# A gated delta-rule mixer: projections cut into halves and emitted between the stages of the inverse and the steps of the scan, decays four heads at a time, squares 512 wide, two output tiles opened in the last scan

## The chip, the cores and the metric

The kernel runs on one core of a Trainium2 chip. A core has a matrix engine (TensorE, "PE" in the profile; "PEld" is its weight load), VectorE ("DVE"), ScalarE ("ACT"), GpSimd ("POOL") and SyncE ("SP"), which run their own streams of instructions and wait for each other by semaphores; transfers between HBM and the on-chip memory SBUF go through queues that SP and POOL fill. The metric is the device time of one launch in microseconds (us). Lower is better. Matrix results land in PSUM, a small memory of eight banks.

## The reference

A trunk of two layers on 512 tokens of width 1024. Each layer is a half-step feed-forward block, a mixer, another half-step feed-forward block, each behind an RMS norm. The first layer's mixer is an attention and convolution hybrid; the second layer's is a gated DeltaNet of eight heads of 128, which alone is touched here. Cut to that:

```python
proj = h @ w_in                                    # q, k, v, z: 8 heads x 128 each; b, a: 8 each
qkv  = silu(causal_depthwise_conv(proj[q, k, v], conv_w))     # 4 taps
beta = sigmoid(b);  g = -exp(a_log) * softplus(a + dt_bias)   # log decay per token and head
# gated_delta_rule(l2_normalize(q), l2_normalize(k), v, g, beta), in chunks:
g     = cumsum(g within a chunk)
decay = exp(where(causal, g[i] - g[j], -inf))
l_mat = where(strict, (k*beta) @ k.T * decay, 0)
t_inv = inverse(l_mat + eye)                       # a triangular inverse per head and chunk
u, w  = t_inv @ (v*beta),  t_inv @ (k*beta*exp(g))
attn  = where(causal, q @ k.T * decay, 0)
for each chunk:                                    # the scan: a state S per head
    v_new = u - w @ S
    o     = (q*exp(g)) @ S + attn @ v_new
    S     = S * exp(g_last) + (k*exp(g_last - g)).T @ v_new
return (rms_norm(o, norm_g) * silu(z)) @ w_out
```

## The kernel before

Everything is float32 to the reader. A product of full accuracy (`mm3`) is made of three matmuls on split operands, high by high, low by high and high by low, at the lines 140, 141 and 142 of the profile. Activations lie transposed: features on the 128 partitions, the 512 tokens along the free axis (`T` = 512, four chunks `c` of 128). A **projection** (`proj`, one head of q, k, v or z) is 8 blocks `k` times 3 matmuls of 128x512, and there are 32 of them. Its weights come by `load_split`: SP loads `raw` from HBM, ACT makes `whi` and `wlo` = -whi (lines 126, 127), and a DMA of POOL's queue adds the weights into `wlo` (line 128, "wlo<-in_wgdn"). `whi` and `wlo` have three buffers each.

Work per pair of heads, in `gdn_heads`:

- `key_pair(pair)`: projections of k, the convolution and SiLU (`conv_silu`; VectorE lines 1034 and 1039, ACT lines 1037 and 1043), transposes on PE (line 1051), sums of squares (`sumsq`, ACT line 1057: for each of four chunks a Square with an accumulator), and after the first pair `decay(hd)` for all eight heads. A `decay` broadcasts a row on PE (line 156), makes `exp` on ACT (1117), a subtraction on VectorE (1120) and four more `exp` on ACT (1122), and stores two tiles to HBM, `Ed` and `Dd`, through POOL's queue (1118, 1123). These tiles are taken from a set of five buffers with the tag `s`, as nearly all passing tiles of the mixer are. Then the pair's `Dd` comes back, k times k is formed (1155), scaled into the strict lower matrix (VectorE, 1158) and stored as `Ld` (1160).
- `substitute(half)`: for four heads at once, 31 rows of forward substitution on VectorE, each a multiply (1178) and a reduction (1179), which invert the 32x32 diagonal blocks. It reads `Ld` and writes `Vd` in HBM (1182).
- `value_query(hd)`: projections of v and q, `vb`, the product q by k (1203), the masked attention `at`.
- `gate(hd)`: the projection of z and its SiLU (1212, 1213).
- `inverse(pair)`: loads `Ld` and `Vd` (1221) and puts the blocks together in four small stages on PE (lines 1229, 1235, 1241/1242, 1249), with VectorE or ACT between.
- `scan(pair)`: four chunks by two heads, each a chain of small matmuls on PE (1263, 1267, 1268, 1273, 1282) with VectorE and ACT between; then sums of squares of the output `po`, a factor `f`, and scaled copies (1298).
- `finish(hd)`: transposes, gate and norm gain (1306), and a split into `o_x[hd]`, an operand of the output projection.
- `out_proj`: eight output tiles `d`, each 8 blocks `k` by 3 matmuls over `o_x[0]` to `o_x[7]`.

The order of instructions within each engine in this part is set by a scheduler at build time: it goes by data and buffers, by its own costs, and by the order in which the code emits the work (earlier is more urgent). It may pull later-emitted work ahead of work that it thinks must wait. Emitted in a row are: keys of pairs 0 and 1, `substitute(0)`, keys of pairs 2 and 3, values and queries of heads 0 and 1, `inverse` of pair 0; then for each pair its `scan`, the next pair's `inverse`, after the first scan `substitute(1)`, the gates of this pair, values and queries of the next, and `finish`. PSUM has two banks for each of the tags `mm`, `po`, `tr` and `sc`.

## Time and profile before

| what | value |
|---|---|
| median of 3 runs | 2097.8 us (2097.16 to 2097.91) |
| the profiled execution, its own time | 2098.93 us |
| its span, first to last instruction | 2097.2 us |
| mean granted TensorE clock | 0.974 of full speed |
| PE busy | 2020.4 us, 96% of the span |
| VectorE busy | 1609.0 us, 77% |
| ScalarE busy | 1113.9 us, 53% |
| the DeltaNet mixer | about 1341 to 1720 us of the span |
| in it, 1341 to 1498 (up to the first inverse) | PE busy 142.24 of 157.00 us, clock 0.97 |
| in it, 1498 to 1585.5 (first inverse to third) | PE busy 80.21 of 87.50 us, clock 0.80 |
| in it, 1585.5 to 1720 | PE busy 134.05 of 134.50 us, clock 0.97 |

A line of a table by windows gives, for a stretch of the span, the busy time of each engine with its count of instructions, then the granted TensorE clock (1.00 is full speed), the busy share of the DMA engines, and what they moved. PE counts as busy too while its matmuls run at a lower clock, so what PE lost is read from both numbers: its idle time, and the clock below 1. A line of a table of waits names the engine and the line that waited, what ended the wait, the sum, the number of times and the longest.

### The profile page before, as it was taken

What the parts mean: (1) busy time and instruction counts of PE and PEld (TensorE: products, weight loads), DVE (VectorE), ACT (ScalarE), POOL (GpSimd) and SP (SyncE); (2) the same over time, 40 slices, a digit from 0 to 9 for tenths busy, and PEclk for the clock granted to TensorE, in tenths of its full rate; (3) what the DMA queues carried; (4) which work ended last, traced back from release to release, by engine and by line L of the source; (5) the groups of instructions that cost most, each with busy time, mean ns of one, the idle gap of its engine ahead of it and who ended that gap; (6) DMA issues with size and microseconds to landing.
All of it is one profiled execution on the core that took longest, in us unless ns stands there. A gap on an engine that the chain in (4) does not pass through costs nothing.

```text
span 2097.2 us, 32970 instructions
## 1 busy us (share of the span) xinstructions
PE 2020.4 (96%) x12694; PEld 1785.7 (85%) x12694; DVE 1609.0 (77%) x2758; ACT 1113.9 (53%) x1981; POOL 134.0 (6%) x190
## 2 busy tenths in 40 slices
PE   7999999999999999998999999979989999999997
PEld 6999998786579999987999998767778878999986
DVE  5888879798567888889888788657585578888876
ACT  5444447547654444465444446676445654444455
POOL 0000000110000000000000000233302210000000
PEclk9999999999899999999999999999889999999998
DMA  3333332784143333322333332679635563333321
GB/s 125 101 103 109 101 100 83 183 194 97 29 101 116 101 104 108 96 86 84 107 104 105 101 101 82 183 215 231 137 106 131 121 132 107 109 101 102 104 87 46
DMA packets 108845, 237.70 MB, mean 113 GB/s; under 512 B 22160, under 2 KB 24976, under 8 KB 108688
## 3 DMA queue, kind: packets, MB, share of 16 engines
q1 hardware_dynamic: 90544, 193.06, 29.7%
q0 software_dynamic: 17616, 42.02, 10.8%
q8 instruction: 99, 1.62, 0.3%
q14 instruction: 58, 0.48, 0.1%
q10 hardware_dynamic: 528, 0.52, 0.1%
HBM read 224.55 MB, written 11.01 MB: 112 GB/s over the span
## 4 chain that ended last, share of the span: by engine, by line
PE 80%; DVE 8%; issue 5%; ACT 3%; DMA 3%; SPq 0%; POOL 0%; DVEq 0%; ACTq 0%; POOLq 0%
PE mm L141 13%; PE mm L140 13%; PE mm L142 13%; PE sc L141 7%; PE sc L140 7%; PE sc L142 7%; PE po L142 3%; PE po L141 2%; PE po L140 2%; PE tr L140 2%; PE tr L142 2%; PE tr L141 2%; DVE wlo L117 1%; DVE gl L386 1%; PE tr L1051 1%
## 5 line engine op out<-in xcount | busy, mean ns | idle before, releaser
L117 DVE TENSOR_TENSOR wlo<-raw,whi 128x1024 fp32r<-128x1024 f32 (+1 forms) x400 | 473.3, 1201 | 158.8 <-ACT whi L116 154.3
L140 PE MATMUL mm<-xh,whi 128*128 128x256 f32 (+2 forms) x1800 | 562.0, 312 | 8.7 <-ACT b L456 4.0
L142 PE MATMUL mm<-xh,wlo 128*128 128x256 f32 (+2 forms) x1800 | 557.9, 310 | 3.0 <-DMA wlo<-in_wgdn 3.0
L141 PE MATMUL mm<-xl,whi 128*128 128x256 f32 (+2 forms) x1800 | 556.3, 309 | 0.0
L116 ACT ACTIVATE whi<-raw 128x1024 fp32r<-128x1024 f32 (+1 forms) x400 | 404.8, 1034 | 33.9 <-issue 14.4
L140 PEld LDWEIGHTS mm<-xh,whi 128*128 128x128 f32 (+1 forms) x1800 | 344.7, 192 | 42.4 <-ACT b L456 7.2
L141 PEld LDWEIGHTS mm<-xl,whi 128*128 128x128 f32 (+1 forms) x1800 | 344.6, 191 | 26.3 <-issue 1.1
L142 PEld LDWEIGHTS mm<-xh,wlo 128*128 128x128 f32 (+1 forms) x1800 | 344.7, 192 | 20.5 <-DMA wlo<-in_wgdn 3.6
L140 PE MATMUL sc<-xh,whi 128*128 128x256 f32 x1056 | 299.8, 284 | 5.8 <-ACT xh L250 3.0
L141 PE MATMUL sc<-xl,whi 128*128 128x256 f32 x1056 | 299.0, 283 | 3.4 <-DVE xl L251 3.4
L142 PE MATMUL sc<-xh,wlo 128*128 128x256 f32 x1056 | 298.8, 283 | 0.9 <-DVE wlo L117 0.8
L140 PEld LDWEIGHTS sc<-xh,whi 128*128 128x128 f32 x1056 | 202.0, 191 | 7.8 <-ACT xh L250 3.6
L141 PEld LDWEIGHTS sc<-xl,whi 128*128 128x128 f32 x1056 | 202.1, 191 | 4.0 <-DVE xl L251 4.0
L142 PEld LDWEIGHTS sc<-xh,wlo 128*128 128x128 f32 x1056 | 202.1, 191 | 1.8 <-DVE wlo L117 1.8
L386 DVE TENSOR_TENSOR gl<-g,gh 128x512 fp32r<-128x512 f32 (+1 forms) x286 | 178.6, 643 | 32.3 <-ACT gh L385 30.0
L385 ACT ACTIVATE gh<-g 128x512 fp32r<-128x512 f32 (+1 forms) x286 | 166.4, 592 | 67.1 <-PE mm L141 34.8
L403 ACT ACTIVATE a<-a 128x512 f32<-128x512 f32 x88 | 55.6, 632 | 253.8 <-DVE a L402 253.8
L126 ACT ACTIVATE whi<-raw 128x512 fp32r<-128x512 f32 (+2 forms) x109 | 77.0, 734 | 97.9 <-PE mm L141 72.0
L442 ACT ACTIVATE b<-mm 128x256 f32<-128x256 f32 x84 | 32.2, 383 | 155.9 <-PE mm L142 155.9
L456 ACT ACTIVATE b<-mm 128x256 f32<-128x256 f32 x88 | 33.7, 383 | 141.0 <-PE mm L142 141.0
L141 PE MATMUL mm<-gl,whi 128*128 128x512 f32 (+1 forms) x220 | 83.1, 378 | 4.9 <-DVE gl L386 4.7
L777 DVE SCALAR_TENSOR_TENSOR cv<-pad,prm_t,cv 128x512 f32<-128x512 f32 x120 | 83.8, 743 | 0.8
(419 smaller groups left out, 3544.8 us busy)
## 6 DMA issues: line engine op xcount, KB each, us to landing
raw<-in_wf1i SPq DMA_DIRECT2D x82, 512.0 KB, 3.6
raw<-in_wf2i SPq DMA_DIRECT2D x82, 512.0 KB, 3.5
raw<-in_wgdn SPq DMA_DIRECT2D x32, 512.0 KB, 5.2
wlo<-in_wgdn POOLq DMA_DIRECT2D x64, 256.0 KB, 6.1
raw<-in_wf2i SPq DMA_DIRECT2D x56, 256.0 KB, 2.6
raw<-in_wf1i SPq DMA_DIRECT2D x52, 256.0 KB, 2.6
raw<-in_wf1b SPq DMA_DIRECT2D x20, 512.0 KB, 3.5
raw<-in_wf2b SPq DMA_DIRECT2D x20, 512.0 KB, 3.5
```

What stands on the lines that cost most here:

```text
L116: A.activation(hi[:, s], src[:, s], AF.Copy)
L117: V.tensor_sub(lo[:, s], src[:, s], hi[:, s].bitcast(F32))
L126: A.activation(hi[:, s], raw[:, s], AF.Copy)
L140: PE.matmul(ps, whi, xhi, start=first, stop=False, skip_group_check=skip)
L141: PE.matmul(ps, whi, xlo, start=False, stop=False, skip_group_check=skip)
L142: PE.matmul(ps, wlo, xhi, start=False, stop=last, skip_group_check=skip)
L385: A.activation(hi, g[f][:, s], AF.Copy)
L386: V.tensor_sub(lo, g[f][:, s], hi.bitcast(F32))
L403: A.activation(cg[f], cg[f], AF.Silu)
L442: A.activation(b0[f][:, HT:], pb[f][:, :HT], AF.Copy)
L456: A.activation(b1[f][:, :HT], pb[f][:, :HT], AF.Copy)
L777: V.scalar_tensor_tensor(acc, x, w, acc, op0=ALU.mult, op1=ALU.add)
```

## The change

Five edits, all in the mixer:

1. `conv_silu`, `key_pair`, `value_query` and `gate` become generators. A projection is emitted as two halves of 12 matmuls (`pieces`), with a place between them where another part of the code may go on. A list `fills` holds such generators, and `fill()` emits one piece of them: five times in each `inverse` and after all but one of the eight steps of each `scan`. The first inverse has `value_query(1)` and `gate(0)` to draw on; each scan and the inverse after it have the open gates and the next pair's values and queries. What is left over is emitted after the inverse, before `finish`.
2. `decay` is called for four heads after the first pair of keys and for the other four after the third, instead of eight after the first.
3. `sumsq` makes one Square of 128x512 on ACT into a new tile `sq`, and one reduction on VectorE, instead of four Squares of 128x128 with accumulators. It is called 24 times.
4. In the last scan, two output tiles (`open_out`) draw their weights and run the blocks `k` = 0 to 5 into two PSUM banks of the tag `mm`; `out_proj` then adds only `k` = 6 and 7 for these two.
5. `value_query(1)` is emitted after the first inverse has begun and no longer ahead of it.

```diff
-            o_x = gdn_heads(xn, op)
+            o_x, opened = gdn_heads(xn, op)
             xn.close()
-            out_proj(io["wgdno"], o_x, nxt, range(NK), ahead)
+            out_proj(io["wgdno"], o_x, nxt, opened, ahead)
...
+            def pieces(idx):
+                wt = load_split(W[idx], 1024)
+                ps = psum("mm")
+                for k in range(NK):
+                    hi, lo = wt[k // 4]
+                    c = slice(k % 4 * P, k % 4 * P + P)
+                    mm3(ps, hi[:, c], lo[:, c], xn.x[k], k == 0, k == NK - 1)
+                    if k == 3:
+                        yield
+                return ps
+
+            def run(*gens):
+                for gen in gens:
+                    for _ in gen:
+                        pass
+
+            fills = []
+
+            def fill():
+                while fills:
+                    try:
+                        next(fills[0])
+                        return
+                    except StopIteration:
+                        fills.pop(0)
 
             def conv_silu(idx, tag, bufs):
-                ps = proj(W[idx], xn)
+                ps = yield from pieces(idx)
...
             def sumsq(ps, ss, hd):
-                for c in range(NT):
-                    junk = gt("junk", 1, n=P)
-                    A.activation(junk, ps[:, ch(c)], AF.Square, accum_out=col(ss, c, hd))
+                sq = tmp("sq", 1)
+                A.activation(sq, ps, AF.Square)
+                V.tensor_reduce(v3(ss)[:, :, hd:hd + 1], c3(sq), axis=AX.X, op=ALU.add)
...
             def key_pair(pair):
                 for hd in pair:
-                    k = conv_silu(8 + hd, "big", 16)
+                    k = yield from conv_silu(8 + hd, "big", 16)
...
-                if pair[0] == 0:
-                    for hd in range(H):
+                if pair[0] % 4 == 0:
+                    for hd in range(pair[0], pair[0] + 4):
                         decay(hd)
...
             def value_query(hd):
-                vT = conv_silu(16 + hd, None, 0)
+                vT = yield from conv_silu(16 + hd, None, 0)
...
                 SP.dma_start(c3(qe[hd]), Ed[:, hc(hd)])
-                qT = conv_silu(hd, "qT", 2)
+                yield
+                qT = yield from conv_silu(hd, "qT", 2)
...
                 A.activation(at[hd], ps, AF.Copy)
+                yield
 
             def gate(hd):
-                pz = proj(W[24 + hd], xn)
+                pz = yield from pieces(24 + hd)
...
                     G.tensor_mul(c3(l1[hd]), c3(ld[hd]), K["lev"][:, None, :].to_broadcast([P, NT, P]))
+                fill()
                 for hd in pair:
                     tb[hd] = gt("s", NS)
...
                         PE.matmul(po[hd][:, ch(c)], at[hd][:, ch(c)], vn, start=(c == 0), stop=True)
+                        if c or hd != pair[0]:
+                            fill()
                 for hd in pair:
                     sumsq(po[hd], sso, hd)
...
             pairs = [(0, 1), (2, 3), (4, 5), (6, 7)]
-            key_pair(pairs[0])
-            key_pair(pairs[1])
+            def open_out(d):
+                wt = load_split(io["wgdno"][d], 1024)
+                ps = psum("mm")
+                opened.append((ps, wt))
+                out_mm(ps, wt, o_x, (0, 1, 2), True, False)
+                yield
+                out_mm(ps, wt, o_x, (3, 4, 5), False, False)
+                yield
+
+            opened = []
+            run(key_pair(pairs[0]), key_pair(pairs[1]))
             substitute(0)
-            key_pair(pairs[2])
-            key_pair(pairs[3])
-            for hd in pairs[0]:
-                value_query(hd)
+            run(key_pair(pairs[2]), key_pair(pairs[3]), value_query(0))
+            fills.extend((value_query(1), gate(0)))
             inverse(pairs[0])
             for p, pair in enumerate(pairs):
+                fills.extend(gate(hd) for hd in pair if hd)
+                if p < 3:
+                    fills.extend(value_query(hd) for hd in pairs[p + 1])
+                else:
+                    fills.extend(open_out(d) for d in range(2))
                 scan(pair)
                 if p < 3:
                     inverse(pairs[p + 1])
                 if p == 0:
                     substitute(1)
-                for hd in pair:
-                    gate(hd)
-                if p < 3:
-                    for hd in pairs[p + 1]:
-                        value_query(hd)
+                run(*fills)
+                fills.clear()
                 for hd in pair:
                     finish(hd)
-            return o_x
+            return o_x, opened
```

Hunks with a lone `fill()` in `inverse` after the first, the loads and `out_proj` are left out; `out_proj` skips for the opened tiles what `open_out` has done.

Three places show how instructions move in the built order. Both orders have the same 20 projections ahead of the first inverse, and neither has any from there until the second scan has begun.

POOL, where the decays are stored. `Ed` and `Dd` are stores of a decay, `Ld` one of a key head, `wlo` the accumulating load of a projection's weights, `pad` a small clear for the convolution. Before, the rows from the ninth store of a decay on:

```order
L1123 DMA Dd<-s_13882 128x512
L1123 DMA Dd<-s_13897 128x512
L1118 DMA Ed<-s_13909 128x512
L1118 DMA Ed<-s_13924 128x512
L128 DMA wlo_14304<-in_wgdn 128x512
L1123 DMA Dd<-s_13912 128x512
L1123 DMA Dd<-s_13927 128x512
L1118 DMA Ed<-s_13939 128x512
L1033 MEMSET pad_14438 128x3
L1160 DMA Ld<-s_13973 128x512
L1123 DMA Dd<-s_13942 128x512
L1160 DMA Ld<-s_13986 128x512
```

Now, from the fourth store of a decay on:

```order
L1152 DMA Dd<-s_13842 128x512
L1147 DMA Ed<-s_13854 128x512
L1147 DMA Ed<-s_13869 128x512
L1152 DMA Dd<-s_13857 128x512
L1152 DMA Dd<-s_13872 128x512
L1062 MEMSET pad_14250 128x3
L128 DMA wlo_14218<-in_wgdn 128x512
L1189 DMA Ld<-s_13903 128x512
L128 DMA wlo_14376<-in_wgdn 128x512
L1189 DMA Ld<-s_13916 128x512
```

The eight stores of the first group are followed by the first pair's `Ld` rows at once; the other eight now stand in one piece further on, behind the two `Ld` rows of the second pair.

PE, from the end of the first inverse into the first scan. Before (the first two rows end the inverse, `sc` and `po` are the scan's):

```order
L1249 MATMUL tr_14892<-s_14879 64x64 x4
L1249 MATMUL tr_14898<-s_14890 64x64 x4
L1268 MATMUL sc_14906<-vb_14616,Vb_14828 128x128
L1268 MATMUL sc_14916<-vb_14747,Vb_14834 128x128
L1273 MATMUL sc_14906<-vk_14909,big_13759 128x128
L1273 MATMUL sc_14916<-vk_14919,big_13819 128x128
L1282 MATMUL po_14904<-vn_14908,at_14695 128x128
L1263 MATMUL sc_14926<-S_14912,big_13752 128x128
L1267 MATMUL po_14904<-S_14912,qe_14623 128x128
L1282 MATMUL po_14905<-vn_14918,at_14826 128x128
L1263 MATMUL sc_14940<-S_14922,big_13812 128x128
L1268 MATMUL sc_14926<-r__2574_14928,Vb_14828 128x128
```

Now, at the same place (`tr` rows of L1080 and L1233 are transposes and the q by k product of `value_query` of heads 1 and 2):

```order
L1080 MATMUL tr_14820<-cst,qT_14818 128x128 x4
L1233 MATMUL tr_14829<-big_13807,qT_14818 128x128 x4
L1080 MATMUL tr_14835<-cst,s_14737 128x128 x4
L1285 MATMUL tr_14842<-s_14785 64x64 x4
L1285 MATMUL tr_14848<-s_14796 64x64 x4
L1305 MATMUL sc_14879<-vb_14576,Vb_14652 128x128
L1080 MATMUL tr_15053<-cst,b_15051 128x128 x4
L1310 MATMUL sc_14879<-vk_14882,big_13759 128x128
L1305 MATMUL sc_14889<-vb_14732,Vb_14658 128x128
L1080 MATMUL tr_15130<-cst,qT_15128 128x128 x4
L1319 MATMUL po_14877<-vn_14881,at_14650 128x128
L1310 MATMUL sc_14889<-vk_14892,big_13814 128x128
```

Groups of four small matmuls of `value_query` now stand between the rows of the inverse and of the scan; projections do not. From the first inverse to the end of the second there are twelve such groups now and none before; eight groups stood just behind the second inverse instead. The four of head 1 have come from ahead of the first inverse.

PE, at the end of the last scan. Before, 19 matmuls of a projection stand behind the last row of the scan (L1282), and then, with `mm_16959` the first output tile and L1051 the transposes of `finish`:

```order
L142 MATMUL mm_16879<-xh_13556,wlo_16883 128x512
L140 MATMUL mm_16959<-hi_15546,whi_16951 128x512
L141 MATMUL mm_16959<-lo_15547,whi_16951 128x512
L142 MATMUL mm_16959<-hi_15546,wlo_16952 128x512
L140 MATMUL mm_16959<-hi_15557,whi_16951 128x512
L1051 MATMUL tr_16917<-cst,vb_16471 128x128 x2
L141 MATMUL mm_16959<-lo_15558,whi_16951 128x512
L1051 MATMUL tr_16917<-cst,vb_16471 128x128
L142 MATMUL mm_16959<-hi_15557,wlo_16952 128x512
L1051 MATMUL tr_16917<-cst,vb_16471 128x128
```

Now, 13 matmuls of the second opened output tile (`mm_16806`) stand behind the last row of the scan (L1319), the last three of them at the top here, then `finish` (L1080), and the blocks 6 and 7 of both opened tiles (`mm_16759` is the first):

```order
L140 MATMUL mm_16806<-hi_16591,whi_16798 128x512
L141 MATMUL mm_16806<-lo_16592,whi_16798 128x512
L142 MATMUL mm_16806<-hi_16591,wlo_16799 128x512
L1080 MATMUL tr_16855<-cst,vb_16256 128x128 x4
L1080 MATMUL tr_16866<-cst,vb_16463 128x128 x4
L140 MATMUL mm_16759<-hi_16862,whi_16751 128x512
L140 MATMUL mm_16806<-hi_16862,whi_16798 128x512
L141 MATMUL mm_16759<-lo_16863,whi_16751 128x512
L142 MATMUL mm_16759<-hi_16862,wlo_16752 128x512
L140 MATMUL mm_16759<-hi_16873,whi_16751 128x512
L141 MATMUL mm_16806<-lo_16863,whi_16798 128x512
```

The transposes of `finish` have no output-projection rows between them any more, and the rows behind them, twelve in all, take `o_x[6]` and `o_x[7]` (`hi_16862` and `hi_16873` with their `lo`) before the third output tile begins.

More of the change, by code (lines that the diff above doesn't have):

```diff
@@ L293, in finish, with out_proj @@
             self.rows()
[L295 removed]
+    def out_proj(w, xs, nxt, opened, ahead):
         nxt.open()
[L297 removed]
+        wt = [o[1] for o in opened]
         for d in range(NK):
[L299 to L307 removed]
+            if d < len(opened):
+                ps = opened[d][0]
+                out_mm(ps, wt[d], xs, (6, 7), False, True)
+                if d == 0:
+                    wt.append(load_split(w[2], 1024))
+            else:
+                ps = psum("po" if d % 2 else "mm")
+                if d < NK - 1:
+                    wt.append(load_split(w[d + 1], 1024))
+                for _ in range((0, 0, 0, 0, 0, 1, 1, 2)[d]):
+                    step(ahead)
+                out_mm(ps, wt[d], xs, range(NK), True, True)
             V.tensor_add(h[d], ps, h[d])
@@ L1236, in inverse @@
                     V.tensor_add(Vb[hd], zz, Vb[hd])
+                fill()
                 for hd in pair:
@@ L1245, in inverse @@
                     A.activation(ts[hd][:64], t64[:64], AF.Copy)
+                fill()
                 for hd in pair:
```

15 lines of the change are left out of this document (4 added, 11 removed).

## The prediction

> **What bounds the kernel now.** I read the page's first part, then a table by windows over the mixer, since the share of the whole span hides its stages, then waits and the chain in the windows where PE falls behind.
>
> ```profile
> PE 2020.4 (96%) x12694; PEld 1785.7 (85%) x12694; DVE 1609.0 (77%) x2758; ACT 1113.9 (53%) x1981; POOL 134.0 (6%) x190
> ```
>
> ```profile
> 1360.00:1380.00 20.00, 20.00 (x123) 17.44 (x123) 11.25 (x28) 19.44 (x48) 7.24 (x15) 1.00 0.57 155
> 1380.00:1400.00 20.00, 13.04 (x67) 10.21 (x65) 10.11 (x20) 16.35 (x44) 6.78 (x12) 0.92 0.74 255
> 1400.00:1420.00 20.00, 16.19 (x71) 12.85 (x70) 12.01 (x47) 10.36 (x32) 7.43 (x11) 0.82 0.97 238
> ...
> 1500.00:1520.00 20.00, 18.60 (x104) 15.31 (x105) 6.67 (x18) 2.65 (x6) 3.48 (x4) 0.66 0.42 83
> 1520.00:1540.00 20.00, 18.21 (x115) 14.85 (x113) 14.11 (x58) 9.59 (x41) 1.27 (x1) 0.75 0.54 184
> 1540.00:1560.00 20.00, 16.10 (x89) 14.55 (x90) 18.32 (x50) 7.36 (x22) 1.27 (x1) 0.74 0.00 1
> ...
> 1580.00:1600.00 20.00, 20.00 (x119) 16.08 (x117) 7.97 (x13) 8.75 (x18) 5.36 (x8) 0.87 1.01 253
> 1600.00:1620.00 20.00, 19.95 (x151) 17.95 (x149) 13.18 (x33) 8.93 (x33) 2.54 (x2) 0.96 0.03 10
> ...
> 1680.00:1700.00 20.00, 20.00 (x87) 16.12 (x86) 11.29 (x20) 12.83 (x23) 6.06 (x8) 1.00 0.88 182
> ```
>
> PE is the bound. The last row is PE undisturbed: 87 matmuls of 128x512 in 20 us, 0.23 us each, clock 1.00. So a gain can only come from windows where PE idles or its clock is down. Busy time times clock gives the work done. Stage A, 1380 to 1420: 13.04 x 0.92 + 16.19 x 0.82 = 25.3 of 40 us, 14.7 lost. Stage B, 1500 to 1560: 18.60 x 0.66 + 18.21 x 0.75 + 16.10 x 0.74 = 37.9 of 60, 22.1 lost, 15.1 of it to the clock and 7.1 to idle time. 1580 to 1620 loses 2.6 + 0.9. That is some 40 us in all, the ceiling of the change.
>
> Stage A is the one with the decays. Its waits, 1360 to 1415, and the stores:
>
> ```profile
> POOL wlo L128 <- ACT junk L1057: 11.7, 5, 6.0
> DVE s L1158 <- DMA s<-Dd: 8.2, 3, 4.9
> POOL Ed L1118 <- ACT s L1117: 4.8, 3, 3.6
> PE sc L1155 <- DVE s L1158: 3.0, 2, 2.7
> PE mm L142 <- DMA wlo<-in_wgdn: 3.0, 2, 2.2
> PE tr L156 <- DVE s L1120: 2.2, 1, 2.2
> ```
>
> ```profile
> L1118 POOL DMA_DIRECT2D Ed<-s x8: 539/539/576, 1367.2 to 1389.2; - x8
> DMA to landing us min/median/max: 2.5/4.3/6.6
> ```
>
> ```profile
> L1123 POOL DMA_DIRECT2D Dd<-s x8: 539/540/861, 1372.3 to 1394.3; - x8
> ```
>
> The sixteen stores take from 1367.2 to 1394.3 to be issued. Each holds one of five `s` buffers until it has landed, 4.3 us in the median. Behind them on POOL stand the weights' `wlo`, for which PE waits (3.0), and the first pair's `Ld`; ACT, busy 19.44 and 16.35 of 20, holds the same `wlo` back by the small squares (11.7).
>
> Stage B is two inverses and two scans with VectorE between. The chain of waits, 1490 to 1590, shows what ends it:
>
> ```profile
> 1491.44 6.20 DMA Vb<-Vd
> 1497.78 2.04 PE tr L1229 x16
> ...
> 1585.47 1.79 PE tr L1229 x16
> ```
>
> ```profile
> L1178 DVE TENSOR_TENSOR sb<-sb,lb 128x2 f32<-128x2 f32 (+30 forms) x31 | 12.0, 386 | 0.4
> L1179 DVE TENSOR_REDUCE sb<-sb 128x1 f32<-128x2 f32 (+30 forms) x31 | 10.4, 337 | 0.4
> L1281 DVE COPY vn<-sc 128x128 f32<-128x128 f32 x8 | 2.3, 282 | 0.6 <-PE sc L1268 0.6
> ```
>
> ```profile
> L1178 DVE TENSOR_TENSOR sb<-sb,lb x31: 149/328/974, 1527.6 to 1563.6; 128x2 f32<-128x2 f32 x1, 128x3 f32<-128x3 f32 x1, 128x8 f32<-128x8 f32 x1, 128x10 f32<-128x10 f32 x1
> ```
>
> `substitute(1)` is 12.0 + 10.4 = 22.4 us of VectorE, yet it lasts from 1527.6 to about 1565, since rows of the second scan stand between its own (in 1540 to 1560 VectorE is busy 18.32 of 20). Then come the stores of `Vd`, the loads of `Vb` and, at 1585.47, the third inverse.
>
> **The change, part by part.**
>
> *Decays by four heads.* The order puts eight stores where sixteen stood, then the first pair's `Ld`. With five buffers, a store waits for an earlier landing from the sixth on: 16 - 5 = 11 times before, 8 - 5 = 3 times in each of the two groups now, 6 of 11. So A keeps 14.7 x 6/11 = 8.0 and gives up 6.7; I take 7. Bounds: nothing, if the second group costs as much as half of the first stage, and 14.7, if both groups hide behind projections.
>
> A switch of ScalarE's function table costs this, from the same stretch:
>
> ```profile
> L1117 ACT ACT_TABLE_LOAD x1 | 1.3, 1283 | 0.0
> ```
>
> The built orders hold as many table loads in the mixer after the change as before, so I count none. A page of the Trainium skill speaks against the split: ScalarE: Activation LUTs, section "Table sets: the hidden batching unit", groups the work of one table set before a switch, and gives one switch about 2.66 us with its drain. By that page a second group of `exp` between SiLUs would cost ScalarE up to 5.3 us, an estimate, and the term would be about -2. The trace agrees on the 1.283 us of the load; it shows no drain beside it.
>
> *Squares.* The old and the new form, from the rows of line 1057 and of two other lines:
>
> ```profile
> L1057 ACT ACTIVATE junk<-tr 128x128 f32<-128x128 f32 x64 | 17.8, 278 | 3.9 <-DVE big L1130 1.5 <-PE tr L1051 1.5
> L1057 ACT ACTIVATION_READ_ACCUMULATOR junk<-tr 128x1 f32 x64 | 13.1, 204 | 0.0
> L260 ACT ACTIVATE sq<-h 128x512 f32<-128x512 f32 x6 | 3.7, 622 | 1.3 <-DVE h L308 1.3
> ```
>
> ```profile
> 1564.47 0.68 DVE L1179 TENSOR_REDUCE sb<-sb 128x16 f32<-128x512 f32 x1
> ```
>
> Per call ACT gives up 4 x (0.278 + 0.204) - 0.622 = 1.3 us and VectorE takes 0.68; over 24 calls 31 us and 16 us. Almost all lies beside PE. In A four calls stand among the decays, 5.2 us less of ACT where it is nearly full; I take 2 of them for PE (between 0 and 5.2), since `wlo` waited for these squares and PE for `wlo`.
>
> *Small groups moved.* The order shows projections in neither version between the first inverse and the second scan, so the fills do not reach the place where PE loses most. What moves is four groups of four matmuls of head 1, from ahead of the first inverse into B. At 2.04 us for sixteen (the chain above) A is 2 us shorter; B has room for them, at worst at half the clock, 4 us. A in all: -7 - 2 - 2 = -11.
>
> *B.* Between the first and last row of `substitute(1)` VectorE now has three of the new reductions, 3 x 0.68 = 2.0 us, besides two copies of 128x128 and rows of the second inverse that came before it. VectorE is saturated there and the third inverse follows its end through two transfers, so this is on the path, with about 1 us for the rows moved in. I take +3. Bounds: -7.1, if the groups take away all idle time, and +7, if the second scan, whose rows start later, drags `substitute(1)` by the 4 us of groups as well.
>
> *Projections and gates spread over scans 2 and 3.* In 1580 to 1620 PE is already busy 20.00 and 19.95. 0, within 1.5.
>
> *Two opened tiles.* The end of the last scan, on ACT and PE:
>
> ```profile
> 1669.74 0.28 ACT L1057 ACTIVATE junk<-po 128x128 f32<-128x128 f32 x1 [1.25 <-PE po L1282]
> ...
> 1672.72 0.20 ACT L1057 ACTIVATION_READ_ACCUMULATOR junk<-po 128x1 f32 x1
> ...
> 1675.17 2.18 ACT L1298 ACTIVATE vb<-po,f 128x128 f32<-128x128 f32 x8 [0.44 <-DVE f L152]
> ```
>
> ```profile
> 1675.59 0.59 PE L1051 MATMUL tr<-cst,vb 128*128 128x128 f32 x2 [0.37 <-ACT vb L1298]
> ```
>
> From the first square to the first transpose it takes 5.85 us, covered by 19 + 4 matmuls x 0.23 = 5.3; PE waited 0.37. The new squares take 2 x 0.622 + 0.68 = 1.9 in place of 3.2, so 4.6 us, but the order leaves 13 matmuls as cover, 3.0: 1.6 us idle. The eight transposes then go at the pace of the scaled copies (2.18 us for eight, against 1.0 for PE) with nothing between them, 1.2 more, and the twelve matmuls of blocks 6 and 7 wait for `finish`, which I put at 0.5. Against 0.37 and some 0.7 before, that is +2; bounds 0 and +5. The weights of the two tiles are loaded under the scan; their cover is its projections.
>
> Sum: -11 + 3 + 0 + 2 = -6, from 2098.93 to 2092.9 for a profiled execution. The median of runs lies 1.1 below that execution: 2091.8, forecast 2092.
>
> **The rivals.**
>
> *A larger gain.* The groups and halves keep PE so busy that the clock stays up in B. A then gives 14.7 + 2 and B 7.1: 2097.8 - 16.7 - 7.1 + 2 = 2076. For it: 15.1 us of B are clock. Against it: no projection stands there in the order. TensorE: Matmul & The Clock Gate, Part 1 of the Trainium skill, says that the clock halves after an idle window of about 3.4 us and returns after a busy one. The trace shows 0.66 at 18.60 us busy, so the rows of small matmuls count for less than their busy time, and the rule gives this rival no more than its idle share.
>
> *Given back.* A gains 11, but B's end hangs on `substitute(1)`, whose own start needs rows of VectorE behind the first scan; with +7 in B and +4 at the end the time is 2097.8. For it: VectorE at 18.32 of 20.
>
> *Slower: the second group of decays stalls PE as all eight did.* It comes right behind the second pair's `Ld` rows on POOL, and the five `s` buffers that its stores hold are then wanted by the reloaded `Dd` and the `Ld` tiles of the neighbouring pairs as well, while the `wlo` of following projections stands behind its eight stores. Say the first group costs half of 14.7, 7.4, and the second 14.7: A is +7.4 - 2 - 2 = +3.4, with +3 and +2 the sum is +8.4, 2106. For it: `Dd` was waited for 8.2 us. Against it: more projections are under way at that place. It ends above 2102 from a second group of 10.5 us on, where A is -0.8.
>
> **How the numbers follow.** What a measurement can tell from no change is 0.2%, 4.2 us: faster is below 2093.6, slower above 2102.0. Forecast 0.43 (its own range 2087 to 2096), larger gain 0.15, given back 0.20, slower rival 0.22 (2102 to 2106). Faster: 0.15 and all but 0.03 of the forecast, 0.55. Same: 0.03 + 0.20 = 0.23; slower 0.22. The range goes from 2080 to 2104: it leaves out about half of the larger gain, whose full 2076 needs every idle microsecond, and half of the slower case.
>
> **What would show it.** Right: the sixteen stores in two pieces, the first inverse near 1487 in place of 1497.78; from there to the third inverse some 90 us in place of 87.7; clock still near 0.7 in B; an idle PE of 1 to 2 us ahead of the transposes of `finish`, then a wait for the split `o_x`; PE undisturbed elsewhere. Wrong: a first inverse at 1495 or later (second group as costly as the first), or a clock near 1 in B, or a third inverse that PE no longer waits for.

## The result, and the profile after

The changed kernel took 2113.64 us in the median of 4 runs (2111.47 to 2115.16) against 2097.74 (2097.16 to 2097.91): ratio 1.0079, 95% interval 1.0065 to 1.0093. The forecast was 2092, range 2080 to 2104. The loss is +16 us.

The same windows as in the prediction, of the changed kernel, and the two stretches behind the first inverse:

```profile
1380.00:1400.00 20.00, 15.72 (x91) 12.92 (x91) 13.30 (x39) 12.38 (x21) 7.18 (x11) 1.00 1.02 272
1400.00:1420.00 20.00, 17.52 (x85) 14.95 (x85) 14.53 (x36) 16.44 (x36) 8.58 (x15) 0.91 0.76 211
...
1440.00:1460.00 20.00, 14.30 (x67) 11.82 (x66) 14.12 (x50) 8.97 (x16) 8.88 (x12) 0.94 0.94 252
...
1480.00:1500.00 20.00, 15.94 (x73) 13.25 (x72) 7.50 (x11) 8.02 (x15) 8.23 (x14) 0.96 0.94 190
1500.00:1520.00 20.00, 16.37 (x93) 13.30 (x92) 5.45 (x12) 5.66 (x13) 2.51 (x2) 0.67 0.41 91
1520.00:1540.00 20.00, 16.91 (x118) 15.58 (x116) 14.43 (x58) 5.74 (x15) 1.42 (x2) 0.84 0.33 117
1540.00:1560.00 20.00, 17.13 (x83) 14.02 (x83) 15.31 (x47) 6.17 (x16) 2.53 (x2) 0.50 0.11 40
...
1680.00:1700.00 20.00, 18.54 (x86) 14.04 (x86) 8.70 (x25) 7.84 (x19) 1.74 (x2) 0.91 0.29 60
```

```profile
1497.90:1595.40 97.50, 87.40 (x472) 73.87 (x473) 61.94 (x174) 37.11 (x87) 13.27 (x16) 0.75 0.39 101
1595.40:1735.20 139.80, 137.72 (x744) 110.84 (x743) 81.38 (x171) 72.14 (x145) 31.04 (x36) 0.96 0.52 117
```

```profile
L1147 POOL DMA_DIRECT2D Ed<-s x8: 539/540/872, 1366.5 to 1407.7; - x8
```

1380 to 1420 got better: 15.72 x 1.00 + 17.52 x 0.91 = 31.7 us of work done there in place of 25.3, with the stores of the decays in two pieces. But 1440 to 1460 and 1480 to 1500, full before the change as these two rows of the kernel before show, now fall to 14.30 and 15.94, and the first inverse starts where it did.

```profile
1440.00:1460.00 20.00, 20.00 (x97) 16.77 (x97) 15.79 (x53) 12.66 (x29) 9.05 (x14) 1.00 0.84 209
1480.00:1500.00 20.00, 19.31 (x93) 15.84 (x91) 10.94 (x18) 11.74 (x21) 10.09 (x17) 1.00 0.91 168
```

What PE, and then VectorE, waited for in the changed kernel, between 1420 and 1500 and between 1430 and 1490:

```profile
PE tr L1080 <- DVE s L1234: 5.7, 1, 5.7
PE tr L1262 <- DMA Vb<-Vd: 4.1, 1, 4.1
```

```profile
DVE s L1234 <- DMA s<-Dd: 2.7, 1, 2.7
DVE s L1187 <- DMA s<-Dd: 2.7, 1, 2.7
```

L1234 is the masked product of `value_query(0)`, and `Vb` is the first inverse's input, written at the end of `substitute(0)`. Before the change PE waited 2.7 us for the masked product and 0.5 for `Vb`. The two rows of VectorE stand between rows of the first substitution: twice it waits for a `Dd` that is loaded back into an `s` buffer, once for a key head (L1187) and once for L1234 itself. So the 5.7 us are a wait for a reload as much as for VectorE's work. The substitution starts earlier, lasts longer and ends at nearly the same time (before, then after):

```profile
L1178 DVE TENSOR_TENSOR sb<-sb,lb x31: 150/327/1208, 1447.3 to 1482.9; 128x2 f32<-128x2 f32 x1, 128x3 f32<-128x3 f32 x1, 128x8 f32<-128x8 f32 x1, 128x10 f32<-128x10 f32 x1
```

```profile
L1207 DVE TENSOR_TENSOR sb<-sb,lb x31: 154/325/1715, 1438.7 to 1480.8; 128x2 f32<-128x2 f32 x1, 128x3 f32<-128x3 f32 x1, 128x8 f32<-128x8 f32 x1, 128x10 f32<-128x10 f32 x1
```

Its last multiply starts 2.1 us earlier than before, but from there to the first inverse, through two transfers, it takes 17.1 us in place of 14.9: the stores of `Vd` land 4.3 us after their issue in the median, 2.7 before.

The table takes starts from each run's trace: the first matmul of the first and of the third inverse, and the last addition to the residual behind the output projection. (In vq_banks only four of the third inverse's first sixteen matmuls start at 1570.9, the others from 1594.3 on.)

| kernel | first inverse | third inverse | last addition | median us | ratio to before, 95% interval |
|---|---|---|---|---|---|
| before | 1497.8 | 1585.3 | 1720.8 | 2097.7 | |
| after | 1497.9 | 1595.4 | 1735.2 | 2113.6 | 1.0079 (1.0065 to 1.0093) |
| decay_alone | 1505.0 | 1590.4 | 1724.6 | 2105.6 | 1.0030 (1.0019 to 1.0041) |
| squares_alone | 1501.3 | 1591.4 | 1727.2 | 2106.5 | 1.0036 (1.0023 to 1.0049) |
| fills_alone | 1504.8 | 1601.2 | 1746.1 | 2124.7 | 1.0108 (1.0086 to 1.0130) |
| open_alone | 1500.8 | 1586.9 | 1733.5 | 2108.6 | 1.0044 (1.0031 to 1.0057) |
| after_decays_off_s | 1496.8 | 1594.2 | 1734.1 | 2119.2 | 1.0093 (1.0060 to 1.0125) |
| before_decays_off_s | 1508.4 | 1594.8 | 1730.3 | 2111.2 | 1.0060 (1.0045 to 1.0076) |
| gates_as_fill | 1496.7 | 1585.8 | 1721.3 | 2102.6 | 1.0024 (1.0006 to 1.0041) |
| no_open | 1498.2 | 1596.1 | 1734.9 | 2114.6 | 1.0064 (1.0040 to 1.0087) |
| sub_cut | 1476.6 | 1571.6 | 1711.7 | 2092.5 | 0.9978 (0.9965 to 0.9990) |
| gates_inplace | 1493.5 | 1584.4 | 1725.0 | 2102.2 | 1.0011 (0.9996 to 1.0027) |
| no_squares | 1501.5 | 1604.8 | 1743.3 | 2123.1 | 1.0116 (1.0090 to 1.0142) |
| before_inplace | 1501.5 | 1589.5 | 1729.0 | 2109.4 | 1.0047 (1.0027 to 1.0067) |
| before_sub_cut | 1481.2 | 1572.0 | 1705.6 | 2082.9 | 0.9921 (0.9898 to 0.9944) |
| before_kk | 1503.9 | 1590.7 | 1724.7 | 2103.2 | 1.0021 (1.0009 to 1.0033) |
| gates_inplace_kk | 1494.8 | 1579.4 | 1720.8 | 2103.3 | 1.0024 (1.0008 to 1.0040) |
| vq_banks | 1479.1 | 1570.9 | 1789.4 | 2174.0 | 1.0355 (1.0323 to 1.0388) |
| decay_lb | 1504.7 | 1590.6 | 1725.9 | 2104.7 | 1.0040 (1.0020 to 1.0061) |
| gates_lb | 1493.3 | 1582.5 | 1718.1 | 2101.5 | 1.0027 (1.0013 to 1.0040) |

By the first three columns the loss of the change is +0.1 up to the first inverse, +10.0 from there to the third (97.5 against 87.5), +4.3 from there to the last addition (139.8 against 135.5), and 1.5 behind it. The kernel before varied from 2091 to 2107 between executions in these comparisons, so single starts a few us apart say little; one execution's trace stands behind each row. In open_alone and after_decays_off_s that execution took 2113.97 and 2113.83 us, some 5 us above and below the median of its kernel.

### The profile page after: what moved, and what is told of

Its sections match the earlier page's. It is cut to its first block, busy times and chain, and to the rows that moved or that the text cites. A ratio compares the mean times of both kernels' runs of the same rounds, so it can differ in the third digit from the quotient of the medians.

```text
span 2113.1 us, 32829 instructions
## 1 busy us (share of the span) xinstructions
PE 2029.1 (96%) x12694; PEld 1792.2 (85%) x12694; DVE 1623.6 (77%) x2782; ACT 1096.8 (52%) x1813; POOL 134.3 (6%) x190
## 5 line engine op out<-in xcount | busy, mean ns | idle before, releaser
L459 ACT ACTIVATE b<-mm 128x256 f32<-128x256 f32 x88 | 33.6, 382 | 140.6 <-PE mm L142 140.6
```

Source lines behind the costliest of these rows:

```text
L459: A.activation(b1[f][:, :HT], pb[f][:, :HT], AF.Copy)
```

## The experiments

The letters in the expectations: P puts the loss at places (the small groups in the second stretch, the first substitution, the end of the last scan); V blames VectorE, by its new reductions or by the length of a substitution; S the second group of decays; B and B2 the five `s` buffers; D transfers; G the groups on an in-order PE; T the two `tr` banks.

**One edit at a time.** Each of the four separable edits alone, on the kernel before.

```diff
-                if pair[0] == 0:
-                    for hd in range(H):
+                if pair[0] % 4 == 0:
+                    for hd in range(pair[0], pair[0] + 4):
```

> The kernel before with one edit: decays four heads at a time. Theory P (places): the split gains ahead of the keys of heads 4 to 7 and hands part of it back before the first inverse; 2092, between 2088 and 2098, the first inverse at 1492 or earlier. Theory V (VectorE's new reductions carry the loss): this edit holds none of them, so it keeps its whole gain, about 2090. Third theory S (the second group of decays stalls PE like the first): 2102 or more.

Slower, 2105.6: no theory's number but the stall theory's. Its place is another, though. The pad product of the seventh and tenth projection starts 12 and 9 us earlier than before, then PE waits between the tenth and the twelfth. Two views of 1420 to 1460 show for what, PE's waits and POOL's:

```profile
PE mm L142 <- DMA wlo<-in_wgdn: 8.2, 3, 5.5
```

```profile
POOL wlo L128 <- ACT junk L1057: 9.2, 2, 7.3
```

The old squares on ScalarE hold back the weights of a projection here. decay_alone and, below, no_squares have old squares and split decays together, and both have this wait; the changed kernel, with new squares, has 1.5 us of it.

```diff
-                for c in range(NT):
-                    junk = gt("junk", 1, n=P)
-                    A.activation(junk, ps[:, ch(c)], AF.Square, accum_out=col(ss, c, hd))
+                sq = tmp("sq", 1)
+                A.activation(sq, ps, AF.Square)
+                V.tensor_reduce(v3(ss)[:, :, hd:hd + 1], c3(sq), axis=AX.X, op=ALU.add)
```

> The kernel before with one edit: one Square of 512 and a reduction on VectorE. Theory P: off the path, 2096 within 3. Theory V: 24 reductions of 0.68 us lengthen both substitutions, 3 to 5 us each, 2104 or more.

2106.5, V's size, and outside P's. The first substitution lasts 3.3 us longer (1446.5 to 1485.4 against 1447.3 to 1482.9 before), as V had it, and PE waits 4.8 us for `Vb` in place of 0.5; the second does not (36.3 against 36.0 us).

fills_alone has the diff of the change without the decays, the squares, `open_out` and `out_proj`.

> The kernel before with the new emission order alone (halves between the stages of the inverse and the scan steps; decays of eight heads, old squares, no opened tiles). Theory P: small groups of value_query between the stages of the first two inverses run at half the clock and lengthen the stretch from the first to the third inverse by about 10 us: 2107, between 2103 and 2112. Theory V: no reductions here, so about 2098 to 2100.

2124.7, the worst of the four and above P's range: 96.4 us between first and third inverse against 87.5, as P expected, but also 7.0 more up to the first, where PE waits 9.2 us for `Vb`, and 9.4 more behind the third, which it did not expect.

```diff
+                if p == 3:
+                    run(gate(6), gate(7))
+                    fills.extend(open_out(d) for d in range(2))
                 scan(pair)
```

> The kernel before with the two opened output tiles alone (the gates of heads 6 and 7 emitted ahead of the last scan, so that nothing but the tiles is left to fill it). Theory P: less cover ahead of finish, 2 to 4 us, 2101. Theory V: less than 1 us, 2098.

2108.6. Slower by more than P said. In the profiled execution the stretch from the first to the third inverse stays (86.1), 3.0 of the loss lie ahead of it and 11.1 behind. There PE waits for the scaled copies ahead of `finish`, four times as long as the changed kernel with its shorter squares:

```profile
PE tr L1080 <- ACT vb L1337: 4.3, 1, 4.3
```

What the rest is stays open. The gates that had filled the last scan stand ahead of it here, so this run does not price the tiles alone; no_open does.

**Leaving one thing out of the change.**

```diff
-                else:
-                    fills.extend(open_out(d) for d in range(2))
```

> The changed kernel without the two opened output tiles (what is left of the gates fills the last scan). Theory P: the cover ahead of finish comes back, 3 us less behind the last scan, 2110. Rival: the tiles only fill what would be idle, and without them the last scan idles more: 2114 to 2118.

2114.6, as the rival had it. From the third inverse to the last addition 138.8 against 139.8: the tiles cost at most about 1 us, less than P's 3 and less than one execution each can tell from nothing, and they are not what the changed kernel lost.

```diff
-                sq = tmp("sq", 1)
...
+                    A.activation(junk, ps[:, ch(c)], AF.Square, accum_out=col(ss, c, hd))
```

> The changed kernel with the old squares (four by accumulator on ScalarE). Theory G (small groups between the stages cost the second stretch): first to third inverse still 95 us or more, 2111 to 2115. Rival V (reductions on VectorE cost it): 91 us or less, 2106.

2123.1, with 103.3 between the inverses. That VectorE's reductions cost the second stretch, as V had it, falls: without them it is longer. Beside the other edits the new squares are worth about 9 us by the medians, though alone they cost some. Ahead of the first inverse PE has the wait for `wlo` shown above again, 8.4 us here in place of 1.5; the inverse comes 3.6 us later, since the wait for `Vb` is gone.

```diff
-            fills.extend((value_query(1), gate(0)))
...
-                fill()          # the five in inverse
...
-                fills.extend(gate(hd) for hd in pair if hd)
-                if p < 3:
-                    fills.extend(value_query(hd) for hd in pairs[p + 1])
+                fills.extend(gate(hd) for hd in pair)
```

> The changed kernel with fills between the scan steps from gates alone (and the opened tiles in the last scan); none between the stages of the inverse, and value_query emitted where it was before. Theory G (the small groups of value_query between the stages cost the second stretch its 10 us): first to third inverse back from 97.5 to 91 or less, 2106. Rival V (the new reductions on VectorE cost it): 95 us or more, 2111 to 2114.

2102.6, and 89.1 us between the inverses, decays, squares and opened tiles still in. So the pieces of `value_query` between the stages of the inverses and the steps of the scans cost the second stretch 8.4 of its 10 us, and 4.3 of what lies behind it too (135.5, as before).

```profile
1496.70:1585.80 89.10, 80.50 (x447) 67.38 (x448) 62.21 (x172) 33.13 (x76) 14.77 (x20) 0.83 0.47 115
```

By this row and the changed kernel's for the same stretch, PE's work, busy time times clock, is nearly equal: 66.8 here, 65.6 there (64.2 before). The changed kernel idles 10.1 us in place of 8.6, and the clock, 0.75 in place of 0.83, takes 21.9 us in place of 13.7. So most of the 8.4 us is clock. (All of `value_query(1)` stands ahead of the first inverse again here, and that inverse still comes at 1496.7, since PE waits there anyhow.) The timeline of PE at the first inverse shows the groups, before and after:

```profile
1497.78 2.02 PE L1229 MATMUL tr<-Vb,s 128*128 128x128 f32 x16 [0.49 <-DMA Vb<-Vd]
1500.58 1.16 PE L1235 MATMUL tr<-s,s 128*128 128x128 f32 x8 [0.78 <-DVE s L1231]
1502.52 1.97 PE L1235 MATMUL tr<-s,s 128*128 128x128 f32 x8 [0.78 <-DVE s L1231]
...
1511.34 1.16 PE L1268 MATMUL sc<-vb,Vb 128*128 128x128 f32 x3
```

```profile
1497.86 3.27 PE L1262 MATMUL tr<-Vb,s 128*128 128x128 f32 x16 [4.07 <-DMA Vb<-Vd]
1501.91 0.66 PE L1080 MATMUL tr<-cst,b 128*128 128x128 f32 x4 [0.79 <-DVE s L1264]
1503.81 1.16 PE L1269 MATMUL tr<-s,s 128*128 128x128 f32 x8 [1.23 <-ACT vb L1222]
1505.75 1.16 PE L1269 MATMUL tr<-s,s 128*128 128x128 f32 x8 [0.78 <-DVE s L1264]
...
1511.09 1.11 PE L1080 MATMUL tr<-cst,qT 128*128 128x128 f32 x4
1512.00 1.92 PE L1233 MATMUL tr<-big,qT 128*128 128x128 f32 x8
1514.75 1.09 PE L1080 MATMUL tr<-cst,s 128*128 128x128 f32 x4 [0.83 <-ACT qT L1072]
...
1517.66 0.58 PE L1305 MATMUL sc<-vb,Vb 128*128 128x128 f32 x1
```

From its first row to the scan's first the inverse takes 19.8 us in place of 13.6. The rows of `value_query` in it take 4.8 us (0.66, 1.11, 1.92 and 1.09), and the waits behind the first row 3.6 in place of 1.6. These groups stand in PE's order ahead of the next stage: one that waits for ScalarE's `qT` holds that stage, a stage waits while ScalarE makes the `vb` copies out of a `tr` bank, and at half clock one group of four costs 1.1 us, not 0.5.

**Which bank?** The same pieces in the `mm` banks.

```diff
-                ps = transposed(vT)
+                ps = transposed(vT, "mm")
...
-                kq = psum("tr")
+                kq = psum("mm")
```

> The changed kernel with the transposes and products of value_query in PSUM banks of the tag mm in place of tr. The built order then has projections between the stages of the first inverses and scans, which neither kernel has. Theory T (the two tr banks, shared with the inverse, are what kept projections out and made PE wait between stages): clock of 0.9 or more between the first and third inverse, 2095 or less. Rival G (on one in-order PE each piece between two stages delays the chain, whatever the bank): the stretch pays for what it hides, 2110 or more.

2174.0, far above T's number. With the built order changed so far that projections do stand in the scans, the clock is back in places, as the last of these rows shows, but PE pays more elsewhere:

```profile
1420.00:1440.00 20.00, 11.85 (x47) 10.21 (x48) 12.41 (x46) 7.86 (x16) 5.67 (x10) 0.76 0.84 206
1440.00:1460.00 20.00, 10.58 (x39) 8.19 (x38) 19.11 (x53) 3.00 (x6) 4.49 (x5) 0.73 0.33 102
1460.00:1480.00 20.00, 11.70 (x45) 9.94 (x46) 9.86 (x16) 6.31 (x13) 5.84 (x10) 0.70 0.76 148
...
1500.00:1520.00 20.00, 19.17 (x118) 15.81 (x117) 14.51 (x54) 8.59 (x19) 5.54 (x8) 1.00 0.74 166
```

```profile
PE mm L1080 <- ACT b L1072: 10.9, 2, 6.3
PE mm L1080 <- DVE s L1234: 6.7, 1, 6.7
```

Between the first and third inverse the clock is 0.87, near T's 0.9, but most of the loss lies behind the third inverse. Theory T falls as a remedy; how much of the 8.4 us is the shared bank and how much the order stays open, since this run changed both.

**What holds the first inverse?** First the buffers.

```diff
-                eg = gt("s", NS)
+                eg = gt("Vb", 4)
...
-                dm = gt("s", NS)
+                dm = gt("Vb", 4)
```

> The changed kernel with the tiles of decay taken from the four Vb buffers, which stand empty until the first inverse, and no longer from the five s buffers. Theory B (the s buffers: with the decays in two groups the reloads of Dd wait for a buffer, and VectorE, in order, waits for them inside the first substitution): the first inverse at 1490 or earlier in place of 1497.9, about 2105. Rival V (VectorE's own work sets the end of the first substitution): first inverse within 2 us of 1498, 2112 to 2114.

> The kernel before with the tiles of decay taken from the Vb buffers. Theory B: the wait for landings and for s buffers at 1380 to 1410 goes, most of the 14.7 us lost there with it, and what it hands back is at most half: 2090, between 2085 and 2094. Rival V: VectorE and ScalarE set the pace of the stage whatever the buffers, 2096 to 2099.

2119.2 and 2111.2: theory B falls as the whole cause. In the changed kernel the wait of PE for L1234 shrank from 5.7 to 1.9 us, waits for `wlo` and `Vb` (3.0 and 4.4) took its place, and the first inverse came at 1496.8. The second kernel took the decays from four buffers where five had been, and lost 11 us up to the first inverse, where PE waited 10.1 us for `Vb`. Since the decays had fewer buffers in both, these runs do not say what a free choice of buffers would give.

```diff
-                for i in range(1, 32):
+                for i in range(1, 32 if hf else 16):
```

> The changed kernel with the first substitution cut to rows 1 to 15 of 31 (the rows 16 to 31 of the diagonal blocks of heads 0 to 3 are left out). Theory V (the end of the first substitution on VectorE holds the first inverse, so what the decays gain waits there): the substitution ends about 12 us earlier and the first inverse comes 4 to 9 us earlier, at 1489 to 1494, as early as PE is done with its 20 projections; 2106. Rival D (transfers or projections themselves set the pace between 1425 and 1498): first inverse within 2 us of 1498, 2112 to 2114.

> The kernel before with the first substitution cut to rows 1 to 15 of 31 (the rows 16 to 31 of the diagonal blocks of heads 0 to 3 are left out). Theory V (the first substitution on VectorE holds the first inverse in the kernel before as well): first inverse at 1485 to 1490 in place of 1497.8, 2086. Rival: before the change PE with its 20 projections set it (PE waited only 0.5 us for Vb there), first inverse at 1496 or later, 2096.

Both leave out rows 16 to 31 of the first substitution, so they are probes and no versions of the kernel. The first matmul of the first inverse, changed kernel and kernel before, each with the cut:

```profile
L1262 PE MATMUL tr<-Vb,s x16: 274/275/276, 1476.6 to 1478.2; 128*128 128x128 f32 x16
```

```profile
L1229 PE MATMUL tr<-Vb,s x16: 274/275/276, 1481.2 to 1482.8; 128*128 128x128 f32 x16
```

21.3 and 16.6 us earlier, more than V expected, and the whole is 21 and 16 us faster. PE does not wait for `Vb` in either. But the cut changed the built order with it: the scheduler left some of the 20 projections for later (the last pad or gate product of those starts behind the first inverse, at 1487.3 and 1507.8). Ahead of the inverse stand about 64 matmuls of projections fewer than the 480 before, some 15 us of PE at 0.23 us each. They now stand between the first and third inverse, where the clock is higher than without them, 0.75 and 0.80 (changed kernel cut, then kernel before cut):

```profile
1476.60:1571.60 95.00, 91.76 (x547) 75.38 (x545) 68.68 (x183) 46.78 (x106) 22.34 (x29) 0.95 0.59 139
1481.20:1572.00 90.80, 90.04 (x527) 75.62 (x526) 64.13 (x174) 50.00 (x142) 24.01 (x32) 0.92 0.64 150
```

So V holds in this form: an earlier end of the first substitution lets the order put the inverse earlier, and the projections left over fill part of the stretch that loses most. The cuts do not show that the substitution alone held PE before. There the 20 projections and the substitution ended almost together, with 0.5 us of wait for `Vb`. In the changed kernel the projections were done 4.1 us ahead of `Vb`, and that wait is the direct evidence that a gain among the decays does not get past it. The wait for L1234 is another matter, for in the cut changed kernel it is as long as without the cut:

```profile
PE tr L1080 <- DVE s L1234: 5.6, 1, 5.6
```

**Looking for a faster version.**

```diff
-                dm = gt("s", NS)
+                dm = at[hd] = gt("at", 4)
...
-                at[hd] = gt("at", 4)
```

> The kernel of gates_as_fill with Dd of value_query loaded into the tile of tag at that later holds the masked attention, and no longer into an s buffer. Theory B2 (value_query waits for an s buffer, and PE for value_query, 6.7 us): that wait goes, first inverse 3 to 6 us earlier than 1496.7, 2098 against 2102.5. Rival V: VectorE's substitution sets the end, first inverse unchanged, 2102.

> The kernel before with Dd of value_query loaded into the tile of tag at. Theory B2: the 2.7 us that PE waited there goes, 2095 to 2097. Rival: nothing, 2098, or a changed order that costs as much as the edits tried so far, 2103.

On gates_as_fill the wait for L1234 went and the first inverse came 3.2 us earlier, but the gain was lost again, most of it behind the third inverse (140.6 against 135.5); the time is the same as gates_as_fill's, and within its interval that of the kernel before. So the wait for L1234 hung on the reload into an `s` buffer, and with it gone PE still waited for `Vb` (2.1). On the kernel before the wait went too, and the time rose to 2109.4.

```diff
-                        V.scalar_tensor_tensor(l[:, ch(c)], kk[:, ch(c)], col(ns, c, hd), dm[:, ch(c)],
+                            A.activation(l[:, ch(c)], kk[:, ch(c)], AF.Copy, scale=col(ns, c, hd))
+                        G.tensor_mul(l, l, dm)          # pairs 2 and 3 only
```

> The kernel before with the scaling of k by k of heads 4 to 7 taken off VectorE (16 operations of 0.35 us between the rows of the first substitution) and done by ScalarE and GpSimd. Theory V: the substitution ends up to 5 us earlier, 2094, between 2091 and 2097. Rival: nothing or worse, 2098 to 2104, since GpSimd's 1.3 us products stand in its queue ahead of wlo.

> The kernel of gates_inplace with the same scaling off VectorE. Theory V: first inverse 3 to 5 us earlier than 1493.5, 2097 against 2102. Rival: first inverse within 2 us of it, 2102.

2103.2 and 2103.3. In the second the substitution ended 2.4 us earlier (its last product 1474.7 against 1477.1) and the first inverse still came at 1494.8, 1.3 later: the rivals' numbers. PE did not wait for `Vb` there but for other things on the way (2.5 for `qT`, 2.3 for `wlo`), so VectorE's substitution is one of two bounds that lie close together.

```diff
-                G.memset(lb.rearrange("p a b -> p (a b)")[:, ::33], 1.0)
+                V.memset(lb.rearrange("p a b -> p (a b)")[:, ::33], 1.0)
```

> The kernel of decay_alone with the small clear of lb (the diagonal of the substitution's matrices) on VectorE, where it no longer stands behind GpSimd's queue of wlo transfers. The built order then ends the first substitution behind the convolution of the 13th projection in place of the 15th. Theory V: first inverse at 1495 or earlier in place of 1505, 2094, a version that is faster than the kernel before. Rival (the stall of PE between the 10th and 12th projection in decay_alone is the bound): first inverse at 1501 or later, 2102 to 2105.

> The kernel of gates_as_fill with the clear of lb on VectorE; the built order ends the first substitution behind the 14th projection. Theory V: first inverse at 1492 or earlier in place of 1496.7, 2097. Rival: first inverse within 2 us of 1496.7, 2102.

The first is bound by the stall of decay_alone (wlo, 6.6 us), as its rival said. In the second the first inverse came at 1493.3, between the two expectations; its time is 1.0027 (1.0013 to 1.0040). No version tried that computes all of it beats the kernel before.

## Why the prediction was wrong

Of the 22 us between the forecast of -6 and the +15.9 of the profiled execution, 11.1 lie in stage A, 7.0 in B, 2.3 from the third inverse to the last addition and 1.5 behind it.

- **"A in all: -7 - 2 - 2 = -11": measured 0 at its end.** The step that failed. The decays and squares, forecast at 9 together, did give 6.4 us more work in 1380 to 1420, and the tenth projection's pad product came at 1426.6 in place of 1434.2. It failed in taking a gain of PE at 1420 for a gain at the first inverse. The prediction quoted the chain with `Vb` ahead of that inverse and read only the second substitution as a bound. In the changed kernel PE waited 4.1 us for `Vb` behind the first substitution and 5.7 for a product whose `Dd` was loaded back late, 3.2 in all at these two places before. Its own sign of being wrong, a first inverse at 1495 or later, came true, but not for the reason that it gave.
- **"B: I take +3", bounds -7.1 to +7: measured +10.0, outside the bounds.** The sign was right, the mechanism wrong. The reductions on VectorE were priced; gates_as_fill, with them, has 89.1 us, 1.6 more than before. The small groups, counted as PE time in free room ("at worst at half the clock, 4 us"), cost 8.4 by gates_as_fill, most of it as clock (0.75 in place of 0.83 over the stretch) and the rest as waits of stages for groups and of groups for ScalarE. How much of this is their place in the order and how much the shared `tr` banks stays open.
- **"Projections and gates spread over scans 2 and 3: 0, within 1.5": measured about +3.** The stretch behind the third inverse lost 4.3, at most about 1 of it the tiles by no_open, and all of it went with gates_as_fill, which has the tiles. Through which wait it was lost stays open.
- **"Two opened tiles: +2": right in mechanism, at most about +1 by no_open.** The timeline shows the three terms (1.6, 1.2 and 0.5 were forecast):

```profile
1692.28 0.39 PE L142 MATMUL mm<-hi,wlo 128*128 128x512 f32 x1
1693.65 2.13 PE L1080 MATMUL tr<-cst,vb 128*128 128x128 f32 x8 [0.98 <-ACT vb L1337]
1696.26 0.73 PE L140 MATMUL mm<-hi,whi 128*128 128x512 f32 x1 [0.48 <-ACT hi L134]
```

  0.98 us wait for `vb`, 2.13 for eight transposes against 1.0 of PE's own pace, 0.48 for the split.
- **"Squares: almost all lies beside PE": wrong in company and alone.** Alone +0.36%, with the first substitution 3.3 us longer; beside the other edits worth about 9 us. An edit off the path changed which of ScalarE's rows stand ahead of a projection's weights.
- **Of the rivals** the slower one named the wrong place: the stores of the second group did not stall PE in the changed kernel, where PE waited 2.3 and 1.5 us between 1395 and 1425. But its reason, that reloaded `Dd` tiles want the five `s` buffers, is part of the 5.7 us wait 40 us later, as gates_inplace shows. "Given back" had the right shape for stage A, with the first substitution in the place of the second. The larger gain was nowhere: the clock in 1540 to 1560 fell to 0.50. The remark against it, that rows of small matmuls count for less than their busy time, is borne out below for some of them.

## What to carry to other kernels

When a stage that loses time is followed by a stage that waits for another engine, find what ends the second one before counting the first one's gain: leaving out part of the suspected work (here half of the substitution) tells whether anything can be had there, if one also looks at what the scheduler moved along with it. Small independent work put between dependent stages of one engine is not free because that engine idles there: each piece brings its own time, its own waits and, here, a lower clock into the chain. And price a bundle together as well as apart, since the four edits alone cost 6 to 26 us each and together 16.

## What the runs showed of the hardware

A long wait costs clock: after a wait of 4.07 us for `Vb` the sixteen matmuls at the head of the first inverse took 3.27 us, against 2.02 after a wait of 0.49. This agrees with what the Trainium skill says in TensorE: Matmul & The Clock Gate, Part 1, on an idle window of about 3.4 us. But waits are not all. In 1540 to 1560 the clock stood at 0.50 with PE busy 17.13 of 20 us and no wait near that length. Inside the changed kernel's second inverse PE was busy all the time, with transposes and products of 64x64 and 128x128, at half the clock (first row). In the kernel before, the rest of the first inverse and the head of the scan ran the same way; right behind them small matmuls alone, mostly of 128x128, had the full clock though PE idled more (second and third row):

```profile
1538.00:1547.00 9.00, 9.00 (x43) 6.86 (x43) 5.43 (x23) 3.70 (x11) 0.00 (x0) 0.50 0.25 87
```

```profile
1502.70:1516.30 13.60, 13.57 (x67) 10.66 (x68) 3.22 (x9) 1.92 (x4) 2.68 (x3) 0.50 0.37 82
1516.30:1530.00 13.70, 12.36 (x96) 10.91 (x95) 9.53 (x35) 4.42 (x20) 0.00 (x0) 1.00 0.37 126
```

So in these traces the clock does not follow PE's busy share. The half-clock stretches hold most of the 64x64 rows; whether these bring it down no run here tests.
